# Sparse attention: a head's value products one turn later, with wide tiles for every other turn's transposed probabilities

## The chip, the cores and the metric

The kernel runs on one core of one Trainium2 chip. The metric is device time in microseconds, the median of several executions. The profile is of one further execution, with the time of every instruction on every engine of the core. TensorE appears in it twice: PE for its matmuls and transposes, PEld for its weight loads. DVE is VectorE, ACT is ScalarE, POOL is GpSimd, SP is SyncE, which here issues DMAs.

## The reference

One decoder layer for 512 tokens of width 1024: a feed-forward block, a token mixer, a second feed-forward block, each with norms and a residual. The mixer adds a native sparse attention (NSA, 8 heads of 64 in two groups) and a dilated attention. The change lies in the NSA part alone. Cut to what matters there:

```python
# s: scaled scores with ALiBi, masked; per head a selected and a window branch
p, _ = masked_softmax(s, mask)          # both branches: all earlier keys, since 512 tokens
o_slc = einsum('bgrqk,bgqkd->bqgrd', p_slc, v_slc)
o_win = banded_attention(q, k_win, v_win, ...)
g = sigmoid(gates)
o_nsa = g[..., 0:1] * o_cmp + g[..., 1:2] * o_slc + g[..., 2:3] * o_win
```

With 512 tokens all blocks of 64 keys are selected and the window holds every earlier key, so both branches are a causal softmax attention over 512 keys, with keys and values of their own. A third branch, over 31 compressed keys, is small.

## The kernel before, in words

All matrix work is done in float32r with an operand split into a rounded part ("hi") and its rest ("lo"): `split` (lines 106 to 108) casts on ACT (L107) and subtracts on DVE (L108). A projection multiplies hi by hi, hi by lo and lo by hi (L130, L131, L132).

The NSA stage is the loop of `nsa` (from L1034). It has 16 items, one for each head and branch (`heads`, L1031: four pairs of heads, two halves, two branches), and it walks them in turns, with one item entering in each turn:

- Turn n, scores: `hb_scores` multiplies queries by keys (L724, L725) into three PSUM banks of the kind S, of 512, 384 + 128 and 256 columns, adds the bias and takes the maximum on DVE (L730), and exponentiates on ACT (L731) into three SBUF tiles.
- Turn n + 2 (`LAG` = 2), probabilities: `hb_probs` scales the item's rows by gate over denominator (ACT L969, POOL L971), transposes them on PE in three blocks (L980, into a PSUM bank of the kind T: 512, 384 + 128 and 256 columns), and splits each block into hi and lo (L984, so L107 and L108), in two of the eight SBUF slots `PT`, each 128 x 512. An item takes six of the eight.
- The same turn n + 2, products: after the scores of the item that enters, `hb_values` multiplies values by the transposed probabilities (L995), for each of the four key blocks first with hi, then with lo, into the one PSUM bank of the kind V. After an item's second branch comes the compressed branch's product (L1061), and `fold` copies and adds the bank into the output (ACT L1003, DVE L1004), which frees the bank V.
- Beside them run a projection for every fourth turn (L130 to L132 into a bank F) and `fillers`: every third turn one projection of the merge gates (`merge_unit`), stored to DRAM.

PSUM has eight banks: three S, two T, one V, two F. So a block's transposes need the bank of the block before the last one, once ACT and DVE have read it, and a group of scores that of three groups back.

The Python order is not the order of the engines. When the program is built, a scheduler lists each engine's instructions: of those whose inputs it reckons ready it takes the one written earliest, so a thing written later fills the holes of what is written before. On the chip each engine then takes its list as it stands and waits on semaphores. The order rows below are those lists.

The tiles `NN` are three SBUF slots of 128 x 1024. Before, they hold token sums in the first feed-forward block, and then, in the dilated part behind NSA, pairs of weight rows for sums made ahead (`mixer_sums`: loads L466, DVE sums L449, stores L470).

Of the kernel before, what the change touches and what calls it, by code (L numbers as in the profile page):

```python
# [13 lines left out]
F32R = mybir.dt.float32r  # L14
# [7 lines left out]
P = 128  # L22
D = 1024
S = 512
# [7 lines left out]
LAG = 2  # L32
# [28 lines left out]
class Layer:  # L61
# [896 lines left out]
                self.softmax_rows(pt[n][:, o:o + ncol], b[:, o:o + ncol], w[:, S - ncol:S], st[:, 0, t:t + 1], st[:, 1, t:t + 1])  # L958
        return st, pt

    def hb_probs(self, st, pt, gate):

        nc = self.nc
        self.gated(st[:, 1], NT, gate)
        for t in (3, 2, 0, 1):
            n, o = self.PLACE[t]
            pp = pt[n][:, o:o + (t + 1) * P]
            if t == NT - 1:
                nc.scalar.mul(pp, pp, st[:, 1, t:t + 1])  # L969
            else:  # L970
                nc.gpsimd.tensor_scalar(pp, pp, st[:, 1, t:t + 1], None, op0=OP.mult)  # L971
        out = {}
        for kbs in ((0,), (1, 3), (2,)):
            b = self.bank("T")
            ncols = 0
            for kk in kbs:
                _, o = self.TPLACE[kk]
                for t in range(kk, NT):
                    pn, po = self.PLACE[t]
                    nc.tensor.transpose(b[:, o + (t - kk) * P:o + (t - kk + 1) * P],  # L980
                                        pt[pn][:, po + kk * P:po + (kk + 1) * P], self.ident)
                    ncols += P
            hi, lo = self.slot("PT", F32R)[:, 0:ncols], self.slot("PT", F32R)[:, 0:ncols]
            self.split(hi, lo, b[:, 0:ncols])  # L984
            for kk in kbs:
                _, o = self.TPLACE[kk]
                c = slice(o, o + (NT - kk) * P)
                out[kk] = hi[:, c], lo[:, c]
        return out
# [16 lines left out]
    def nsa(self, fillers):  # L1006
        nc = self.nc
        ident = lambda v: v
        r = self.wcols([(C_KC, 256)])
        src = [r[:, :, 0:P], r[:, :, P:2 * P]]  # L1010
        r2 = self.wcols([(C_KS, P), (C_KW, P)])
        src2 = [r2[:, :, 0:P], r2[:, :, P:2 * P]]
        early = []
        for s, tag in zip(src + src2, "FFSV"):
            w = self.wslots(s, "SP") if tag == "V" else None
            early.append(self.proj_T(s, self.bank(tag), (0, 2 * P), w))
            if len(early) in (2, 3):
                self.pending.pop(0)()
        for n, (b, w) in enumerate(early):
            self.proj_T(None, b, (2 * P, S), w)  # L1020
        rows = [self.block_rows(b) for b, _ in early[:2]]
        kw = early[3][0]
        vw = self.v_weights()
        kparts = [self.k_parts(early[2][0], ident)]
        gs = [self.blocks(0, rows[0])]
        kparts.append(self.k_parts(kw, ident))
        gs.append(self.blocks(1, rows[1]))
        self.v_nsa(vw)
        early = self.hidden_early(0)
        self.oh, self.ol = [], []  # L1030
        heads = [(i, half, br) for i in range(4) for half in range(2) for br in range(2)]  # L1031
        qs, cmps, ws, live = {}, {}, {}, {}
        probs = {}
        for n in range(len(heads) + LAG):  # L1034
            if n < len(heads) and n % 4 == 0:
                i = n // 4
                b, _ = self.proj_T(self.wcols([(i * 64, 64), (256 + i * 64, 64)]))
                qs[i] = self.q_parts(b, ident)
                if i:
                    cmps[i] = self.cmp_pair(i, qs[i])  # L1040
            m = n - LAG
            if m >= 0:
                i, half, br = heads[m]
                probs[m] = self.hb_probs(*live.pop(m), self.gate[:, :, (i + 4 * half) * 3 + 1 + br])
            if n < len(heads):
                i, half, br = heads[n]
                h = i + 4 * half
                if br == 0:
                    ws[h] = self.slot("W")
                    nc.vector.tensor_scalar(ws[h], self.dm, -(2.0 ** -(h + 1)), None, op0=OP.mult)  # L1050
                kb, ka = kparts[br]
                live[n] = self.hb_scores(qs[i][half], ka[half], kb, half, ws[h])
            if m >= 0:
                i, half, br = heads[m]
                if br == 0:
                    out = self.bank("V")
                    if half == 0:
                        of = self.slot("of")
                self.hb_values(probs.pop(m), br, half, out, br == 0)
                if br == 1:  # L1060
                    nc.tensor.matmul(out, self.vcs[half], cmps[i], start=False, stop=True, skip_group_check=True)  # L1061
                    self.fold(of, half, out[0:64], out[64:128])
                    if half == 1:
                        hi, lo = self.slot("x", F32R), self.slot("x", F32R)
                        self.split(hi, lo, of)
                        self.oh.append(hi)
                        self.ol.append(lo)
            if n < 2:
                self.hidden(n, gs[n], early)
                if n == 0:  # L1070
                    early = self.hidden_early(1)
                else:
                    hid = self.gelu()
            if n == 2:
                self.compressed(hid)
                cmps[0] = self.cmp_pair(0, qs[0])
            fillers()
# [465 lines left out]
```

## Time and profile before

| | |
|---|---|
| median of three runs | 1134.36 us (1134.22 to 1134.58) |
| the profiled execution's own time | 1135.51 us |
| its span, first to last instruction | 1133.7 us |
| outside the span | 1.8 us |
| granted TensorE clock, mean | 0.999 |
| NSA loop, from the first scores to the last value products | about 398 to 533 us of the span |
| instructions of L995, and the first and the last | 128, at 416.1 and 532.5 us |
| transposes L980, and the first and the last | 160, at 413.7 and 530.9 us |

In the rows of a timeline the first column is the start in us of the span, the second the length; an entry in square brackets is the time that the engine sat idle before the instruction, and whose end let it go. A merged row (x2, x4) spans its instructions.

### The profile page before, as it was taken

To read this page: it belongs to the slowest core of one execution; us is meant where nothing else is said; L and a number is where in the kernel's file an instruction comes from. 1 tells how busy PE (TensorE), PEld (TensorE's weight loads), DVE (VectorE), ACT (ScalarE), POOL (GpSimd) and SP (SyncE) were. 2 spreads that over 40 slices of the span, in tenths; PEclk is the share of its full clock that TensorE was granted. 3 is DMA by queue.
4 is the path that set the end of the run, shared out by engine and by line. 5 is a ranking of instruction groups with operands and counts; after the bars stand their busy time and mean duration, and the time that the engine had idled before them with its cause. 6 is when DMAs were issued, how large, how long until landed. Compare 5 with 4: busy or idle time off the path is not lost.

```text
span 1133.7 us, 18456 instructions
## 1 busy us (share of the span) xinstructions
PE 1119.2 (99%) x6921; PEld 1001.7 (88%) x6921; DVE 907.2 (80%) x1563; ACT 638.1 (56%) x1145; POOL 76.8 (7%) x112
## 2 busy tenths in 40 slices
PE   9999999999999999999999999999999999999997
PEld 7889999998888987778888998787989999998886
DVE  6989999879676889687665687986778888979774
ACT  5435555567563788677565634645445555557562
POOL 1000000000012033343000000000000000000000
PEclk9999999999999999999999999999999999999999
DMA  9996665588763542111476758683233424357862
GB/s 320 328 305 194 182 209 173 155 273 287 266 204 96 176 131 85 54 40 56 140 251 224 253 177 292 210 290 118 66 121 122 131 86 127 124 170 239 285 224 84
DMA packets 152908, 206.01 MB, mean 182 GB/s; under 512 B 19794, under 2 KB 97906, under 8 KB 152564
## 3 DMA queue, kind: packets, MB, share of 16 engines
q1 hardware_dynamic: 152816, 204.85, 55.7%
q8 instruction: 54, 0.88, 0.3%
q14 instruction: 34, 0.28, 0.1%
q10 hardware_dynamic: 4, 0.00, 0.0%
HBM read 165.45 MB, written 39.37 MB: 181 GB/s over the span
## 4 chain that ended last, share of the span: by engine, by line
PE 89%; DVE 5%; ACT 2%; issue 1%; DMA 1%; POOL 1%; SPq 0%; POOLq 0%; DVEq 0%; ACTq 0%
PE pb_F L132 11%; PE pb_F L130 11%; PE pb_F L131 11%; PE pb_S L132 8%; PE pb_S L131 8%; PE pb_S L130 8%; PE pb_T L130 6%; PE pb_T L132 6%; PE pb_T L131 6%; PE pb_V L131 3%; PE pb_V L130 3%; PE pb_V L132 3%; PE pb_V L995 2%; PE pb_T L980 1%; DVE SP_s L730 1%
## 5 line engine op out<-in xcount | busy, mean ns | idle before, releaser
L107 ACT CAST whi<-raw 128x1024 fp32r<-128x1024 f32 (+1 forms) x215 | 219.9, 1023 | 251.9 <-issue 68.2
L108 DVE TENSOR_TENSOR wlo<-raw,whi 128x1024 fp32r<-128x1024 f32 (+1 forms) x215 | 255.0, 1188 | 94.9 <-ACT whi L107 91.3
L130 PE MATMUL pb_F<-xh_t,whi 128*128 128x512 f32 (+1 forms) x392 | 142.7, 364 | 0.4 <-ACT whi L107 0.4
L132 PE MATMUL pb_F<-xh_t,wlo 128*128 128x512 f32 (+1 forms) x392 | 141.6, 361 | 0.5 <-DVE wlo L108 0.5
L131 PE MATMUL pb_F<-xl_t,whi 128*128 128x512 f32 (+1 forms) x392 | 141.8, 362 | 0.0
L107 ACT CAST whi<-tmp_t 128x1024 fp32r<-128x1024 f32 x51 | 53.5, 1048 | 60.9 <-PE pb_S L131 22.0
L132 PEld LDWEIGHTS pb_F<-xh_t,wlo 128*128 128x128 f32 x392 | 74.1, 189 | 10.8 <-DVE wlo L108 1.0
L130 PEld LDWEIGHTS pb_F<-xh_t,whi 128*128 128x128 f32 x392 | 74.1, 189 | 10.4 <-ACT whi L107 0.6
L131 PEld LDWEIGHTS pb_F<-xl_t,whi 128*128 128x128 f32 x392 | 74.2, 189 | 9.6
L108 DVE TENSOR_TENSOR wlo<-tmp_t,whi 128x1024 fp32r<-128x1024 f32 x51 | 62.4, 1223 | 25.2 <-ACT whi L107 23.9
L130 PE MATMUL pb_S<-xh_t,whi 128*128 128x256 f32 (+1 forms) x240 | 73.2, 305 | 0.0
L132 PE MATMUL pb_S<-xh_t,wlo 128*128 128x256 f32 (+1 forms) x240 | 73.0, 304 | 0.0
L131 PE MATMUL pb_S<-xl_t,whi 128*128 128x256 f32 (+1 forms) x240 | 73.0, 304 | 0.0
L130 PE MATMUL pb_T<-xh_t,whi 128*128 128x256 f32 (+1 forms) x184 | 54.5, 296 | 0.0
L132 PE MATMUL pb_T<-xh_t,wlo 128*128 128x256 f32 (+1 forms) x184 | 54.3, 295 | 0.0
L131 PE MATMUL pb_T<-xl_t,whi 128*128 128x256 f32 (+1 forms) x184 | 54.3, 295 | 0.0
L152 POOL TENSOR_TENSOR rs_t<-rs_t,mhalf_t 128x1 f32<-128x1 f32 x24 | 17.5, 727 | 542.7 <-DVE rs_t L148 542.7
L971 POOL TENSOR_SCALAR SP_s<-SP_s,st_t 128x384 f32<-128x384 f32 (+2 forms) x48 | 45.8, 970 | 107.1 <-DVE st_t L907 77.3
L131 PEld LDWEIGHTS pb_S<-xl_t,whi 128*128 128x128 f32 x240 | 45.9, 191 | 1.9
L130 PEld LDWEIGHTS pb_S<-xh_t,whi 128*128 128x128 f32 x240 | 45.9, 191 | 1.9
L132 PEld LDWEIGHTS pb_S<-xh_t,wlo 128*128 128x128 f32 x240 | 45.9, 191 | 1.9
L108 DVE TENSOR_TENSOR PT_s<-pb_T,PT_s 128x512 fp32r<-128x512 f32 (+1 forms) x72 | 39.2, 559 | 6.3 <-ACT PT_s L107 5.6
(822 smaller groups left out, 3363.8 us busy)
## 6 DMA issues: line engine op xcount, KB each, us to landing
raw<-in_ffn_w_up_dram SPq DMA_DIRECT2D x36, 512.0 KB, 5.3
raw<-in_w_in_dram SPq DMA_DIRECT2D x18, 1024.0 KB, 5.7
raw<-in_ffn_w_gate_dram SPq DMA_DIRECT2D x35, 512.0 KB, 4.9
raw<-in_ffn_w_down_dram SPq DMA_DIRECT2D x14, 1024.0 KB, 5.7
raw<-tdram SPq DMA_DIRECT2D x14, 1024.0 KB, 5.2
NN_s<-in_ffn_w_down_dram SPq DMA_DIRECT2D x22, 512.0 KB, 5.0
tdram<-NN_s SPq DMA_DIRECT2D x22, 512.0 KB, 3.9
raw<-in_ffn_w_down_dram SPq DMA_DIRECT2D x6, 768.0 KB, 5.8
```

The costliest lines, as they stand in the source:

```text
L107: self.last_cast = self.nc.scalar.copy(dsthi, src).ins
L108: self.last_rest = self.nc.vector.tensor_sub(dstlo, src, dsthi.bitcast(F32)).ins
L130: mm(out, lhi, rhi, start=start, stop=False, skip_group_check=skip)
L131: mm(out, lhi, rlo, start=False, stop=False, skip_group_check=skip)
L132: mm(out, llo, rhi, start=False, stop=stop, skip_group_check=skip)
L152: nc.gpsimd.tensor_tensor(out=r, in0=v, in1=self.mhalf, op=OP.pow)
L730: nc.vector.tensor_tensor_reduce(p, s, w, -1.0, FLOOR, OP.add, OP.min, st_m)
L971: nc.gpsimd.tensor_scalar(pp, pp, st[:, 1, t:t + 1], None, op0=OP.mult)
L980: nc.tensor.transpose(b[:, o + (t - kk) * P:o + (t - kk + 1) * P], pt[pn][:, po + kk * P:po + (kk + 1) * P], self.ident)
L995: self.nc.tensor.matmul(out[:, kk * P:S], v, pp, start=first and kk == 0 and pi == 0, stop=False, skip_group_check=True)
```

## The change

The value products of an item are written one turn later, behind the next item's transposes and scores, so the loop has one turn more. Since the transposed probabilities of two items are now alive together, every other item (the first, the third, and so on) puts its hi and lo side by side in the three wide `NN` tiles; the others keep the `PT` slots.

```diff
-    def hb_probs(self, st, pt, gate):
+    def hb_probs(self, st, pt, gate, wide):
...
-            hi, lo = self.slot("PT", F32R)[:, 0:ncols], self.slot("PT", F32R)[:, 0:ncols]
+            if wide:
+                both = self.slot("NN", F32R, (P, D))
+                hi, lo = both[:, 0:ncols], both[:, S:S + ncols]
+            else:
+                hi, lo = self.slot("PT", F32R)[:, 0:ncols], self.slot("PT", F32R)[:, 0:ncols]
...
-        for n in range(len(heads) + LAG):
+        for n in range(len(heads) + LAG + 1):
...
             m = n - LAG
-            if m >= 0:
+            if 0 <= m < len(heads):
                 i, half, br = heads[m]
-                probs[m] = self.hb_probs(*live.pop(m), self.gate[:, :, (i + 4 * half) * 3 + 1 + br])
+                probs[m] = self.hb_probs(*live.pop(m), self.gate[:, :, (i + 4 * half) * 3 + 1 + br], m % 2 == 0)
...
                 live[n] = self.hb_scores(qs[i][half], ka[half], kb, half, ws[h])
+            m -= 1
             if m >= 0:
                 i, half, br = heads[m]
                 if br == 0:
```

The same instructions stand in both programs. PE's list differs only inside the NSA loop, some 640 matmuls of 6,921; those of DVE and ACT likewise; POOL's by one memset; SP's by three loads. Lines behind the change carry higher numbers: L995 is now L999, L1061 is L1066.

PE, the fifth item. Before, from the last transpose of its first block (bank pb_T_5065) to the first product that reads that block's hi (PT_s_5070):

```order
L980 MATMUL pb_T_5065<-ident_t_61,SP_s_4925 128x128
L980 MATMUL pb_T_5074<-ident_t_61,SP_s_4927 128x128
L980 MATMUL pb_T_5074<-ident_t_61,SP_s_4926 128x128
L980 MATMUL pb_T_5074<-ident_t_61,SP_s_4925 128x128 x2
L724 MATMUL pb_S_5175<-KA_s_4205,Q_s_4851 128x256
L725 MATMUL pb_S_5175<-KB_s_4201,Q_s_4851 128x256
L131 MATMUL pb_F_5197<-xl_t_3671,whi_5193 128x512
L132 MATMUL pb_F_5197<-xh_t_3670,wlo_5194 128x512
L130 MATMUL pb_F_5197<-xh_t_3670,whi_5193 128x512
L131 MATMUL pb_F_5197<-xl_t_3671,whi_5193 128x512
L995 MATMUL pb_V_5115<-PT_s_5070,V_s_4259 128x512
```

After, the end of the stretch before the same products. NN_s_5049, NN_s_5057 and NN_s_5063 hold the fifth item's three blocks, transposed some rows above this piece; pb_T_5113 and pb_T_5122 are the sixth item's banks:

```order
L132 MATMUL pb_F_5177<-xh_t_3670,wlo_5174 128x512
L980 MATMUL pb_T_5113<-ident_t_61,SP_s_5007 128x128
L130 MATMUL pb_F_5177<-xh_t_3670,whi_5173 128x512
L980 MATMUL pb_T_5113<-ident_t_61,SP_s_5008 128x128
L980 MATMUL pb_T_5113<-ident_t_61,SP_s_5007 128x128
L980 MATMUL pb_T_5113<-ident_t_61,SP_s_5006 128x128
L980 MATMUL pb_T_5122<-ident_t_61,SP_s_5008 128x128
L980 MATMUL pb_T_5122<-ident_t_61,SP_s_5007 128x128
L980 MATMUL pb_T_5122<-ident_t_61,SP_s_5006 128x128 x2
L999 MATMUL pb_V_5161<-NN_s_5049,V_s_4259 128x512 x2
L999 MATMUL pb_V_5161<-NN_s_5057,V_s_4288 128x384 x2
L999 MATMUL pb_V_5161<-NN_s_5063,V_s_4317 128x256 x2
```

The fifth item's products have moved behind the sixth item's transposes, and now stand in one piece.

PE, the fourth item. Its third block takes the bank that its first block had. Before, the rows behind the last transpose of the first block (pb_T_4995) up to the first of the third (pb_T_5013):

```order
L724 MATMUL pb_S_5161<-KA_s_4205,Q_s_4851 128x512
L725 MATMUL pb_S_5161<-KB_s_4201,Q_s_4851 128x512
L995 MATMUL pb_V_4947<-PT_s_4919,V_s_4317 128x256
L995 MATMUL pb_V_4947<-PT_s_4911,V_s_4346 128x128
L995 MATMUL pb_V_4947<-PT_s_4912,V_s_4346 128x128
L980 MATMUL pb_T_5004<-ident_t_61,SP_s_4787 128x128
L980 MATMUL pb_T_5004<-ident_t_61,SP_s_4786 128x128
L980 MATMUL pb_T_5004<-ident_t_61,SP_s_4785 128x128 x2
L995 MATMUL pb_V_4947<-PT_s_5000,V_s_4259 128x512
L724 MATMUL pb_S_5166<-KA_s_4205,Q_s_4851 128x384
L725 MATMUL pb_S_5166<-KB_s_4201,Q_s_4851 128x384
L980 MATMUL pb_T_5013<-ident_t_61,SP_s_4786 128x128
```

After, from the last transpose of the first block (pb_T_4980) to the first of the third (pb_T_4998):

```order
L980 MATMUL pb_T_4980<-ident_t_61,SP_s_4772 128x128
L980 MATMUL pb_T_4989<-ident_t_61,SP_s_4774 128x128
L980 MATMUL pb_T_4989<-ident_t_61,SP_s_4773 128x128
L980 MATMUL pb_T_4989<-ident_t_61,SP_s_4772 128x128 x2
L999 MATMUL pb_V_5028<-NN_s_4896,V_s_4288 128x384
L999 MATMUL pb_V_5028<-NN_s_4902,V_s_4317 128x256 x2
L999 MATMUL pb_V_5028<-NN_s_4896,V_s_4346 128x128 x2
L724 MATMUL pb_S_5086<-KA_s_4172,Q_s_4837 128x256
L725 MATMUL pb_S_5086<-KB_s_4168,Q_s_4837 128x256
L980 MATMUL pb_T_4998<-ident_t_61,SP_s_4773 128x128
```

Less PE work stands between the two users of the bank than before.

SP, at the end of the loop. Before (raw are weights for the dilated part, gdram the fillers' stores, tdram the store of finished sums):

```order
L682 DMA raw_6306<-in_w_in_dram 128x8x256
L1086 DMA gdram_3872<-ring_s_5529 128x512
L1086 DMA gdram_3872<-ring_s_5837 128x512
L1086 DMA gdram_3872<-ring_s_6043 128x512
L682 DMA raw_6356<-in_w_in_dram 128x8x256
L682 DMA raw_6358<-in_w_in_dram 128x8x256
L470 DMA tdram_72<-NN_s_6340 128x1024
```

After, the same place:

```order
L682 DMA raw_6282<-in_w_in_dram 128x8x256
L1091 DMA gdram_3872<-ring_s_5504 128x512
L1091 DMA gdram_3872<-ring_s_5804 128x512
L1091 DMA gdram_3872<-ring_s_6010 128x512
L466 DMA NN_s_6316<-in_ffn2_w_down_dram 128x1024
L466 DMA NN_s_6317<-in_ffn2_w_down_dram 128x1024
L682 DMA raw_6332<-in_w_in_dram 128x8x256
L466 DMA NN_s_6484<-in_ffn2_w_down_dram 128x1024
L682 DMA raw_6334<-in_w_in_dram 128x8x256
```

Three loads of the NN tiles have come here from the end of the first feed-forward block, since the tiles are in use until the last wide item's products are done.

## The prediction

> **What bounds the kernel now.** I read the page's first part, then the windows around the NSA loop, then PEld's groups inside that loop, and last the timeline at three waits.
>
> ```profile
> PE 1119.2 (99%) x6921; PEld 1001.7 (88%) x6921; DVE 907.2 (80%) x1563; ACT 638.1 (56%) x1145; POOL 76.8 (7%) x112
> ```
>
> The windows (columns: PE, PEld, DVE, ACT, POOL busy, granted clock, DMA share, GB/s) are the whole loop, a dense stretch of it, and the dilated part behind it:
>
> ```profile
> 396.00:535.00 139.00, 137.46 (x786) 111.71 (x784) 114.42 (x338) 106.50 (x256) 48.41 (x54) 1.00 0.26 77
> 440.00:460.00 20.00, 19.66 (x117) 15.59 (x116) 17.97 (x60) 18.21 (x47) 11.14 (x12) 1.00 0.20 66
> 535.00:560.00 25.00, 25.00 (x118) 20.90 (x117) 16.66 (x36) 14.47 (x31) 1.04 (x2) 1.00 0.37 127
> ```
>
> TensorE is the bound, and a matmul's record covers short waits, so PE's 1.5 us of idle in the loop understates them. The weight loads show more. Their groups in the window 396 to 535 us (busy, mean ns, then idle before them and its releasers):
>
> ```profile
> L995 PEld LDWEIGHTS pb_V<-PT_s,V_s 128*128 128x128 f32 x128 | 21.1, 188 | 8.1 <-ACT PT_s L107 4.0 <-DVE PT_s L108 1.4 <-DVE of_s L1004 0.7
> L980 PEld LDWEIGHTS pb_T<-ident_t,SP_s 128*128 128x128 f32 x160 | 18.2, 141 | 4.4 <-DVE PT_s L108 1.8 <-PE pb_F L130 0.6 <-issue 0.4
> L724 PEld LDWEIGHTS pb_S<-KA_s,Q_s 128*128 128x128 f32 x64 | 12.1, 189 | 3.2 <-DVE st_t L730 1.6 <-issue 0.7 <-DVE Q_s L717 0.2
> ```
>
> The products L995 wait most: 4.0 us for casts (hi), 1.4 us for rests (lo), 0.7 us for the bank V, 6.1 us together. The transposes wait 1.8 us for a bank T, the scores 1.6 us for DVE's L730, which frees a bank S. One such wait, the fifth item's first product, on PEld, on PE and on ACT:
>
> ```profile
> 453.27 0.19 PEld L131 LDWEIGHTS pb_F<-xl_t,whi 128*128 128x128 f32 x1
> 453.92 0.19 PEld L995 LDWEIGHTS pb_V<-PT_s,V_s 128*128 128x128 f32 x1 [0.46 <-ACT PT_s L107]
> 454.03 0.19 PEld L132 LDWEIGHTS pb_F<-xh_t,wlo 128*128 128x128 f32 x1
> ```
> ```profile
> 453.04 0.40 PE L132 MATMUL pb_F<-xh_t,wlo 128*128 128x512 f32 x1
> 453.27 0.39 PE L130 MATMUL pb_F<-xh_t,whi 128*128 128x512 f32 x1
> 453.50 0.39 PE L131 MATMUL pb_F<-xl_t,whi 128*128 128x512 f32 x1
> 453.95 0.47 PE L995 MATMUL pb_V<-PT_s,V_s 128*128 128x512 f32 x1
> 454.26 0.39 PE L132 MATMUL pb_F<-xh_t,wlo 128*128 128x512 f32 x1
> ```
> ```profile
> 452.50 0.58 ACT L1003 COPY of_s<-pb_V 64x512 f32<-64x512 f32 x1
> 453.10 0.59 ACT L107 CAST PT_s<-pb_T 128x512 fp32r<-128x512 f32 x1
> 453.58 0.62 ACT L731 ACTIVATE SP_s<-SP_s,st_t 128x384 f32<-128x384 f32 x1
> ```
>
> Matmuls of 512 columns start 0.23 us apart (453.04, 453.27, 453.50). From 453.50 to 454.26 are 0.76 us for two, 0.30 us lost for 0.46 us of idle on PEld. So two thirds of a PEld wait are lost, and all of L995's are worth about 0.67 x 6.1 = 4.1 us. The weight load behind the waiting one came after it, at 454.03. The Trainium skill (TensorE: Matmul & The Clock Gate, "Step-by-step: what each phase is for") says that PE's window pulls weight loads ahead of matmuls in flight. If that reached past a load that waits, the next load, 0.11 us here, would be hidden and the price 0.19 us, not 0.30; by it the gains below would be 1.4 us, not 2.3. The row decides for 0.30.
>
> **The change part by part.** No instruction is added or removed, and PE's list differs in the loop alone. So only waits change.
>
> *Products against their casts (gain).* The spacing of PE's matmuls in a stretch without a wait:
>
> ```profile
> 439.28 0.39 PE L725 MATMUL pb_S<-KB_s,Q_s 128*128 128x512 f32 x1
> 439.51 0.33 PE L724 MATMUL pb_S<-KA_s,Q_s 128*128 128x384 f32 x1
> 439.68 0.34 PE L725 MATMUL pb_S<-KB_s,Q_s 128*128 128x384 f32 x1
> 439.85 0.22 PE L724 MATMUL pb_S<-KA_s,Q_s 128*128 128x128 f32 x1
> 439.91 0.27 PE L725 MATMUL pb_S<-KB_s,Q_s 128*128 128x128 f32 x1
> 440.02 0.33 PE L724 MATMUL pb_S<-KA_s,Q_s 128*128 128x256 f32 x1
> 440.19 0.28 PE L725 MATMUL pb_S<-KB_s,Q_s 128*128 128x256 f32 x1
> 440.31 0.40 PE L130 MATMUL pb_F<-xh_t,whi 128*128 128x512 f32 x1
> ```
>
> That is 0.23 us for 512 columns (439.28 to 439.51), 0.17 for 384, 0.12 for 256 (440.19 to 440.31) and 0.11 for 128 (439.91 to 440.02). In PE's lists I count the matmul work between a block's last transpose and the first product that reads it, at this spacing, for the 48 blocks (16 items of three). A hi part that waits looks like this one, with 0.55 us of work behind its transposes:
>
> ```profile
> 435.57 0.19 PEld L995 LDWEIGHTS pb_V<-PT_s,V_s 128*128 128x128 f32 x1 [0.25 <-ACT PT_s L107]
> ```
>
> Before, 20 of 48 hi parts have under 1.1 us of work between, and none over 3.1. After, 11 have under 1.1, and 13 over 3.5. The list is therefore only half of what the title says: the scheduler still fills holes with products as soon as it reckons them ready. I let the 4.0 us shrink with the near ones: 4.0 x 9/20 = 1.8 us saved (bounds 0 and 4.0, since waits like the one at 453.92 come from ACT's queue with 1.6 us of work between). Lo parts under 1.7 us fall from 14 to 3: 1.4 x 11/14 = 1.1 us. The bank V: in four items before, at most 2.1 us of work stands between L1061 and the next user, in one after: 0.7 x 3/4 = 0.5 us. Together 3.4 us on PEld, times 0.67: 2.3 us.
>
> *Transposes against their bank (cost).* What leaves the place between two blocks brings their transposes closer. A bank T of 512 columns:
>
> ```profile
> 492.53 0.38 PE L980 MATMUL pb_T<-ident_t,SP_s 128*128 128x128 f32 x2
> ```
> ```profile
> 493.56 0.69 DVE L108 TENSOR_TENSOR PT_s<-pb_T,PT_s 128x512 fp32r<-128x512 f32 x1 [0.22 <-ACT PT_s L107]
> ```
> ```profile
> 493.70 0.42 PEld L980 LDWEIGHTS pb_T<-ident_t,SP_s 128*128 128x128 f32 x4
> 494.31 0.20 PEld L980 LDWEIGHTS pb_T<-ident_t,SP_s 128*128 128x128 f32 x2 [0.19 <-DVE PT_s L108]
> ```
>
> Here 1.45 us of work stood between and 0.19 us was missing, so such a bank needs about 1.6 us. Before, two are under that, both at 1.45. After, five are: 1.22, 1.30 (the fourth item, shown above), 1.41, 1.46 and 1.58. The shortfalls are 0.38 + 0.30 + 0.19 + 0.14 + 0.02 = 1.0 against 0.3 us: 0.7 us more (bounds: 0, if ACT and DVE come earlier than in these rows; 2.6, if in two of five of the banks of the second rival the cast comes late).
>
> *Scores against their bank (cost).* The group of 512 columns that ends with the L725 at 439.28 leaves its bank to the group that starts here:
>
> ```profile
> 440.75 0.19 PEld L724 LDWEIGHTS pb_S<-KA_s,Q_s 128*128 128x128 f32 x1 [0.24 <-DVE st_t L730]
> ```
>
> With 1.26 us of work between it lost 0.1 us, so I take 1.35 us as the need. Before, this is the shortest of its kind; after, two stand at 0.80 and 0.98: 0.55 + 0.37 - 0.09 = 0.8 us more (bounds 0 and 1.5).
>
> *SP's list (no cost).* The three NN loads wait at SP for the last wide products, near the end of the loop, and the two raw loads stand behind them. Before:
>
> ```profile
> 530.19 9.54 SPq L682 DMA_DIRECT2D raw<-in_w_in_dram  x2
> ```
> ```profile
> 547.89 1.06 ACT L107 CAST whi<-raw 128x1024 fp32r<-128x1024 f32 x1 [1.97 <-PE pb_F L131]
> ```
> ```profile
> 544.68 1.41 DVE L449 TENSOR_TENSOR NN_s<-NN_s 128x512 f32<-128x512 f32 x2
> ```
> ```profile
> raw<-in_w_in_dram SPq DMA_DIRECT2D x18, 1024.0 KB, 5.7
> NN_s<-in_ffn_w_down_dram SPq DMA_DIRECT2D x22, 512.0 KB, 5.0
> ```
>
> The first raw tile is issued at 530.19 and cast at 547.89, 17.7 us later, and lands in 5.7 us. The sums that read NN come at 544.68, 14.5 us after that time, and an NN load lands in 5.0 us. If all three came one after another ahead of the raw tile (15 us) and PE's cover of some 12 us were gone, that would cost up to 9 us; I give it 2 in 100. DVE's and ACT's lists change as PE's does, with the same work.
>
> *The sum.* -2.3 + 0.7 + 0.8 = -0.8 us. The profiled execution took 1135.51 us, 1.8 us more than its span of 1133.7, and lies 1.15 us above the median of 1134.36; it would come to 1134.7, the median to **1133.6**. What a measurement of this kernel can tell from no change is about 0.2%, or 2.27 us.
>
> **The rivals.**
>
> *All of L995's waits go and nothing takes their place* (faster). Then the median is 1134.36 - 4.1 = 1130.3. For it: the 13 blocks with over 3.5 us cannot wait for a cast, and in the loop DVE is busy 114 and ACT 107 of 139 us, so they are not full. Against it: 11 blocks stay near. Chance 0.25.
>
> *The bank waits grow by more than the product waits shrink* (slower). The mechanism is the pair of T banks: the third block of an item needs the first one's, 1.6 us after its transposes. After the change 14 banks of 512 columns have at most 1.8 us between, before 10. In the dense stretch ACT is busy 18.21 of 20 us, and the cast has to stand behind an exponential of 0.62 us (453.58). If casts come that much later than in the row above, the 14 lack about 0.6 us each where the 10 now lack little more than the 1.8 us that the view shows, so up to 0.6 x 14 - 1.8 = 6.6 us; with half of them so, 3.3 us more, which leaves 3.3 + 0.8 - 2.3 = +1.8, and with two thirds 2.6 us, or 1137.0. It decides from half on. The Trainium skill (Perfetto Trace Analysis, "Optimization Strategy") has the rule for it: the same gap over and over on the engine that should be full can mean too few SBUF or PSUM buffers. The change adds room in SBUF and none in PSUM; by that rule the gap stays. Chance 0.13.
>
> *The change hardly does what it says* (no change). The scheduler reorders, and in PE's list the last head's products end within 1 us of work of where they did. Then 1134.4. Chance 0.17. My forecast has 0.45.
>
> **How the numbers follow.** The likeliest is 1133.6. The low end is the first rival's 1130.3; the high end takes both costs at their upper bounds with the gain as it is (-2.3 + 2.6 + 1.5 = +1.8, so 1136.2). Left out are half of the slower rival, SP, and a little below. Faster by over 0.2% (below 1132.1): the first rival and the lower tail of the forecast, 0.27. Slower (above 1136.6): 0.13. The rest, 0.60, is within 0.2%.
>
> **What would show it.** In PEld's groups of the same window L999 should show about 2.7 us of named waits in place of 6.1, L980 about 2.5 behind L108 in place of 1.8, L724 about 2.4 behind L730 in place of 1.6; the rest of the span should keep its lengths, and no wait for NN or raw should appear behind 530 us. L999 near zero with the others as they were means the first rival; L980 above 5 us the second; all as before the third.

## The result: 6.3 us slower, and the profile after

| | before | after |
|---|---|---|
| median, runs on the same chip | 1134.47 us (1133.88 to 1135.14) | 1140.76 us (1139.15 to 1143.11) |
| profiled execution, its span | 1135.51, 1133.7 us | 1141.66, 1139.9 us |

The ratio is 1.0056 (95% interval 1.0046 to 1.0066). The forecast was 1133.6 with a range up to 1136.2, and 0.60 of its chances lay on no change: it was wrong.

Where it arose. PE's list differs in the NSA loop alone, so the same matmul can be looked up in both traces by its number. Just before the loop's first changed matmul the execution after is 0.18 us ahead, at its last 5.96 us behind (538.61 for 532.65 us), and at the end of the span 6.15. These are the windows of the kernel after, with the stretch 520 to 540 added (busy PE, PEld, DVE, ACT, POOL, granted clock, DMA share, GB/s):

```profile
396.00:535.00 139.00, 132.30 (x758) 108.06 (x756) 110.29 (x334) 104.36 (x253) 50.13 (x54) 0.99 0.23 67
440.00:460.00 20.00, 17.57 (x102) 14.43 (x102) 16.05 (x53) 15.51 (x41) 7.03 (x6) 0.91 0.21 66
520.00:540.00 20.00, 17.67 (x98) 13.69 (x99) 11.92 (x31) 11.78 (x27) 6.59 (x8) 1.00 0.23 78
535.00:560.00 25.00, 24.84 (x117) 20.32 (x116) 13.85 (x20) 10.59 (x17) 0.00 (x0) 1.00 0.68 224
```

PE is idle for 2.4 us of 440 to 460 (0.34 before), and the granted clock there is 0.91 (1.00 before). PEld's groups of the window 396 to 540:

```profile
L980 PEld LDWEIGHTS pb_T<-ident_t,SP_s 128*128 128x128 f32 x160 | 18.4, 144 | 12.9 <-POOL SP_s L971 5.7 <-issue 2.3 <-DVE NN_s L108 1.7
...
L724 PEld LDWEIGHTS pb_S<-KA_s,Q_s 128*128 128x128 f32 x64 | 12.1, 189 | 2.9 <-DVE st_t L730 1.1 <-issue 0.9 <-DVE Q_s L717 0.2
L999 PEld LDWEIGHTS pb_V<-NN_s,V_s 128*128 128x128 f32 x64 | 10.8, 201 | 2.9 <-ACT NN_s L107 1.8 <-DVE of_s L1008 0.4
L999 PEld LDWEIGHTS pb_V<-PT_s,V_s 128*128 128x128 f32 x64 | 10.4, 190 | 1.3 <-ACT PT_s L107 0.4
```

The products' named waits are 2.6 us, as foreseen (2.7, from 6.1). The scores' are 1.1 (2.4 foreseen). The transposes' waits behind the rest L108 are 3.5 us (2.5 foreseen): 1.7 for NN, shown above, and in the list of waits 1.2 for PT and 0.6 for CP. New is the first entry of L980: 5.7 us for POOL's scaling L971, a releaser that PEld's groups of before do not name at all. All but 0.2 us of it comes at two places. The first is the sixth item (item 5, counted from 0); the timeline after, then before:

```profile
451.93 0.16 DVE L907 TENSOR_TENSOR st_t<-st_t,gate_t 128x4 f32<-128x4 f32 x1
...
452.28 3.17 POOL L971 TENSOR_SCALAR SP_s<-SP_s,st_t 128x384 f32<-128x384 f32 x3 [7.37 <-DVE st_t L906]
...
454.16 0.14 PEld L980 LDWEIGHTS pb_T<-ident_t,SP_s 128*128 128x128 f32 x1 [1.88 <-POOL SP_s L971]
...
455.50 1.36 PEld L980 LDWEIGHTS pb_T<-ident_t,SP_s 128*128 128x128 f32 x7 [1.09 <-POOL SP_s L971]
...
456.84 2.06 PEld L999 LDWEIGHTS pb_V<-NN_s,V_s 128*128 128x128 f32 x7
```
```profile
450.85 0.16 DVE L907 TENSOR_TENSOR st_t<-st_t,gate_t 128x4 f32<-128x4 f32 x1
...
451.20 5.78 POOL L971 TENSOR_SCALAR SP_s<-SP_s,st_t 128x384 f32<-128x384 f32 x6 [6.62 <-DVE st_t L907]
...
457.07 0.86 PEld L980 LDWEIGHTS pb_T<-ident_t,SP_s 128*128 128x128 f32 x8
```

Read them as a chain. An item's rows are scaled by gate over denominator before they are transposed: DVE's three gate steps (L905, L906, L907) come first, then POOL's three scalings, and the first transpose needs POOL's second, the second transpose POOL's third. Before, the scalings of item 5 begin at 451.20 (the merged row holds items 5 and 6) and the transposes come at 457.07, 3.2 us after the third had ended. After, POOL begins 1.1 us later, but PE is there already when its matmul before is done, at 452.4 (452.21 and 0.23 us of spacing). It stands 1.7 us, runs one transpose and one matmul, stands 1.0 us more, and the products L999 of the item before, whose last input DVE had finished at 453.6, are queued behind. The second place is item 14, again after, then before:

```profile
524.47 0.15 DVE L907 TENSOR_TENSOR st_t<-st_t,gate_t 128x4 f32<-128x4 f32 x1
...
524.79 5.44 POOL L971 TENSOR_SCALAR SP_s<-SP_s,st_t 128x384 f32<-128x384 f32 x6 [3.99 <-DVE st_t L905]
...
526.67 0.14 PEld L980 LDWEIGHTS pb_T<-ident_t,SP_s 128*128 128x128 f32 x1 [1.88 <-POOL SP_s L971]
...
527.57 0.75 PEld L980 LDWEIGHTS pb_T<-ident_t,SP_s 128*128 128x128 f32 x7 [0.65 <-POOL SP_s L971]
```
```profile
517.76 2.73 POOL L971 TENSOR_SCALAR SP_s<-SP_s,st_t 128x384 f32<-128x384 f32 x3 [1.07 <-DVE st_t L907]
...
525.15 0.91 PEld L980 LDWEIGHTS pb_T<-ident_t,SP_s 128*128 128x128 f32 x7
```

Before, POOL was 4.7 us early here (517.76 + 2.73 = 520.49, for 525.15). The pauses of item 5 also cost clock. Windows of 2 us after:

```profile
452.00:454.00 2.00, 0.60 (x4) 0.28 (x3) 1.72 (x8) 1.90 (x4) 1.72 (x2) 1.00 0.00 0
454.00:456.00 2.00, 1.06 (x5) 0.75 (x6) 0.66 (x3) 0.00 (x0) 1.45 (x2) 0.81 0.00 0
456.00:458.00 2.00, 2.00 (x9) 1.81 (x9) 0.90 (x3) 1.56 (x4) 0.00 (x0) 0.50 0.00 0
458.00:460.00 2.00, 2.00 (x13) 1.87 (x12) 1.24 (x4) 1.12 (x5) 0.00 (x0) 0.84 0.00 0
```

Behind them the clock stands at 0.50, and PE takes 0.21 us for a transpose (0.11 at full clock), so the seven transposes need 1.36 us where those at 527.57 need 0.75. Against the spacing of the prediction's rows, PE loses 1.7 + 1.0 us in the pauses of item 5, 1.5 at half clock, and 1.7 + 0.7 in the pauses of item 14: 6.6 us, of which the rest of the loop gives 0.5 back. That is the loss.

Why the chain was met there shows in the lists, with the spacings of PE and DVE's durations (0.66 us for 512 columns, 0.54, 0.41, 0.27 for 384, 256, 128, 0.16 for a small step):

| | PE work from the item's last score to its first transpose | DVE work from its last maximum to its last gate step |
|---|---|---|
| item 5, before and after | 14.7, 11.0 us | 6.5, 8.8 us |
| item 14, before and after | 12.2, 10.7 us | 4.2, 10.9 us |

The products that left the place between an item's scores and its transposes let the transposes move up; and in DVE's new list rests (L108) and bias work (L730) stand ahead of the gate steps. Why the scheduler set them there was not followed. Item 5 loses 3.7 + 2.3 = 6.0 us of a margin of 3.2, item 14 1.5 + 6.7 = 8.2 of 4.65. The deficits are 2.8 and 3.5 us; the pauses that PE shows are 2.7 and 2.4. At items 9 and 13 the same count gives deficits of 1.3 and 1.0 us, and PE lost 0.2 us or less there: the count finds tight places, but gives their size only roughly.

### The profile page after: what moved, and what is told of

The parts are those of the page before. It is cut to its first block, busy times and chain, and to the rows that moved or that the text cites. A ratio compares the mean times of both kernels' runs of the same rounds, so it can differ in the third digit from the quotient of the medians.

```text
span 1139.9 us, 18451 instructions
## 1 busy us (share of the span) xinstructions
PE 1119.8 (98%) x6921; PEld 1002.6 (88%) x6921; DVE 905.9 (79%) x1563; ACT 637.8 (56%) x1145; POOL 78.5 (7%) x112
## 4 chain that ended last, share of the span: by engine, by line
PE 89%; DVE 4%; ACT 3%; DMA 1%; issue 1%; POOL 1%; SPq 0%; POOLq 0%; DVEq 0%; ACTq 0%
PE pb_F L132 11%; PE pb_F L130 11%; PE pb_F L131 11%; PE pb_S L130 8%; PE pb_S L131 8%; PE pb_S L132 8%; PE pb_T L130 6%; PE pb_T L132 6%; PE pb_T L131 6%; PE pb_V L130 3%; PE pb_V L131 3%; PE pb_V L132 3%; PE pb_T L980 1%; PE pb_V L999 1%; PE pb_S L724 1%
## 5 line engine op out<-in xcount | busy, mean ns | idle before, releaser
L108 DVE TENSOR_TENSOR wlo<-raw,whi 128x1024 fp32r<-128x1024 f32 (+1 forms) x215 | 255.5, 1190 | 101.9 <-ACT whi L107 99.1
L108 DVE TENSOR_TENSOR wlo<-tmp_t,whi 128x1024 fp32r<-128x1024 f32 x51 | 62.4, 1223 | 25.2 <-ACT whi L107 23.9
L971 POOL TENSOR_SCALAR SP_s<-SP_s,st_t 128x384 f32<-128x384 f32 (+2 forms) x48 | 47.5, 1005 | 110.7 <-DVE st_t L907 55.8
L730 DVE CUSTOM_DVE_ANT_0 SP_s<-pb_S,W_s 128x128 f32<-128x128 f32 (+2 forms) x92 | 37.8, 441 | 6.7 <-PE pb_S L725 4.7
```

Of the source, the lines that this page charges most:

```text
L108: self.last_rest = self.nc.vector.tensor_sub(dstlo, src, dsthi.bitcast(F32)).ins
L730: nc.vector.tensor_tensor_reduce(p, s, w, -1.0, FLOOR, OP.add, OP.min, st_m)
```

## The experiments

The theory, A: the loss is the chain from the gate steps over POOL's scaling to the transposes at these places. Rivals: B, the banks T and S, with casts that come late (the prediction's slower rival); C, the wide tiles themselves. In the kernels with an early scaling, the code below it moves down some lines: their transposes are L984 and their products L1003.

**The gate and the scaling one turn earlier.**

```diff
+            if 2 < n <= len(heads):
+                i, half, br = heads[n - 1]
+                self.hb_scale(*live[n - 1], self.gate[:, :, (i + 4 * half) * 3 + 1 + br])
             m = n - LAG
```

`hb_scale` holds the lines L964 to L971 of `hb_probs`; items 0 and 1 keep theirs. On the kernel after:

> Theory A (the gate steps L905 to L907 and POOL's scaling L971 of items 5 and 14 come after PE has reached these items' transposes): with the gate and the scaling of items 2 to 15 written one turn earlier, DVE has 3.5 us (item 5) and 5.7 us (item 14) of work between the item's last maximum and its last gate step, where the changed kernel has 8.8 and 10.9; the transposes stay where they were (11.9 and 10.8 us of PE work behind the item's last score, 11.0 and 10.7 in the changed kernel). PEld's wait for POOL (5.7 us in the changed kernel) falls under 0.7 us, and the time to 1133 to 1135 us. Rival B (banks T and S, casts late behind exponentials): nothing of it is touched, so 1139 to 1141. Rival C (the wide tiles themselves): 1139 to 1141.

Measured: 1134.89 us, ratio to the kernel before 0.9998 (0.9988 to 1.0008). The named wait for POOL is 1.2 us in three pieces, over the 0.7 expected; but the scaling ended 1.7 us or more ahead of the second transpose in every item, so there POOL's name stands for another releaser. Theory A stands, B and C as causes of the 6 us fall. On the kernel before:

> The kernel before with the same early gate and scaling. Theory A: the kernel before has no wait for POOL, so there is nothing to take away: 1133.5 to 1135. If early scaling is a gain of its own, whatever the products do, it falls by as much as the changed kernel does with it, some 6 us, to about 1128.

Measured: 1135.42 us, 1.0008 (0.9999 to 1.0018), 0.4 us above theory A's range. Early scaling is no gain of its own; it only repairs what the change broke.

**The gate steps alone earlier**, with `self.gated(...)` in that place and the scaling left in `hb_probs`:

> The changed kernel with only DVE's three gate steps (L905 to L907) of items 2 to 15 written one turn earlier; POOL's and ACT's scaling stays where it was written. Theory A1 (the link is DVE's list: POOL stands idle until the last gate step has run): DVE has 3.5 and 5.7 us of work between the last maximum and the last gate step of items 5 and 14 (8.8 and 10.9 in the changed kernel), POOL starts that much sooner, its wait on PEld is under 0.7 us and the time 1134 to 1136 us. Theory A2 (the link is POOL's or ACT's scaling itself, where it stands or how long it takes): 1139 to 1141 us.

Measured: 1135.33 us, 1.0010 (1.0001 to 1.0019), as A1 says: the link is DVE's list. The wait for POOL that is left, 2.1 us in five pieces of at most 0.6, is more than the 0.7 expected, yet POOL ended 2.7 us or more ahead of the second transpose in all items but the first (0.05): in the others the name again stands for another releaser.

**Items 5 and 14 alone**, so `if n - 1 in (5, 14)` in the first diff:

> The changed kernel with the early gate and scaling for items 5 and 14 alone. Their transposes stand even a little sooner behind the scores than in the changed kernel (10.5 us both, for 11.0 and 10.7), all other items as there. If the whole loss lies at these two places, the time is 1134.5 to 1136.5 us, and the granted clock, which falls to 0.50 behind the first pause of the changed kernel, stays at 1.00 there. If the loss comes from all the items with late gates (9, 10 and 13 too), it stays over 1137.

Measured: 1134.80 us, 1.0000 (0.9990 to 1.0009). In this execution the transposes of items 5 and 14 begin sooner, at 450.75 and 519.77 us. PEld's group of the transposes, and windows at the two places:

```profile
L984 PEld LDWEIGHTS pb_T<-ident_t,SP_s 128*128 128x128 f32 x160 | 17.8, 141 | 8.5 <-issue 3.0 <-DVE NN_s L108 1.3 <-DVE PT_s L108 1.2
```
```profile
450.00:452.00 2.00, 1.84 (x13) 1.67 (x14) 1.94 (x6) 1.98 (x6) 0.27 (x1) 1.00 0.00 0
452.00:454.00 2.00, 2.00 (x16) 1.83 (x15) 1.92 (x6) 2.00 (x7) 0.00 (x0) 1.00 0.00 0
...
520.00:522.00 2.00, 1.85 (x16) 1.53 (x15) 1.44 (x5) 1.56 (x4) 1.20 (x1) 1.00 0.00 0
```

POOL is gone from the first three releasers, PE is idle for at most 0.16 us in any of these windows, and the clock stays at 1.00. Two items of sixteen carry the whole loss.

**The wide tiles alone**, the products in their old turn (`m -= 1` and the extra turn taken out):

> The wide tiles for every other item, but the products in the turn where the kernel before has them. Theory A and rival B: 1134 to 1135.5, no wait for POOL, since transposes stand as far behind the scores as before (12.2 us at the least). Rival C: the wide tiles cost by themselves, 1137 to 1141.

Measured: 1136.18 us, 1.0011 (1.0002 to 1.0021), no named wait for POOL. Rival C falls as the cause of 6 us; the 1.3 us over the kernel before (at most 2.4 by the interval) is more than I expected. In its trace PE loses 1.3 us more in front of the products than before, and these wait 7.1 us by name for ACT's casts (4.0 before); why the casts come later was not followed.

**Late products, written ahead of the next item's transposes**, that is, the block under `if m >= 0` moved ahead of `hb_probs`:

> The changed kernel, but an item's products, still one turn later, written ahead of the next item's gate, scaling and transposes instead of behind its scores. PE then has at least 12.4 us of work between an item's last score and its first transpose (10.7 in the changed kernel), 14.0 for item 5 and 13.0 for item 14, and DVE 4.2 and 7.4 us before their last gate step. Theory A: no wait for POOL, some of the waits for casts gone: 1132.5 to 1134.5. Rival B: as many transposes as before stand close on each other (3 under 1.6 us where the changed kernel has 9), so it also says at most 1135; rival C (wide tiles): 1139 to 1141.

Measured: 1135.41 us, 1.0004 (0.9994 to 1.0013), no named wait for POOL, with the same lateness and the same tiles. The time is 0.9 us over what was expected: the products' waits for ACT's casts are back (2.9 us for tiles PT, 1.9 for NN), so nothing is gained either.

**A rule from the lists, tried forward.** The block put between `hb_probs` and `hb_scores`:

> The changed kernel, with an item's late products written ahead of the next scores instead of behind them (still behind the next item's gate, scaling and transposes). A rule worked out from the lists is tried on it: take the time by which POOL was early in the kernel before (3.2 us for item 5, 4.8, 4.9 and 4.65 for 9, 13 and 14), add the PE work and subtract the DVE work by which the lists differ from those of the kernel before. For the changed kernel that gives -2.9, -1.3, -1.0 and -3.6 us, and PE stood 2.8, 0.1, 0.1 and 2.4. Here it gives -1.1 (item 5: transposes 3.5 us sooner, gate 0.8 us later), -1.3, -1.0 and -3.6: a pause of about 1.1 us at item 5 with the clock at 1.00 behind it, and the same 2.4 at item 14, so 1137 to 1139.5 us. If lateness as such costs the 6 us, 1140 to 1142.

Measured: 1137.87 us, 1.0024 (1.0014 to 1.0033), the clock 1.00 at both places. PE lost 0.4 us at item 5 and 2.4 at item 14: the rule has the places, and is off by 0.7 us at the first. At the second it counts 3.6, as for the kernel after; the 2.4 was expected from that kernel's pause, not from the rule. Next, the products of items 4 and 13 back in their old turn:

> The changed kernel with the products of items 4 and 13 alone back in their old turn; these are the products that stood queued behind the waiting transposes of items 5 and 14. By the rule from the lists the waits stay (-2.9 us for item 5 as before, -2.9 for item 14, which was -3.6), so 1139 to 1141 us, and the clock falls behind the pause of item 5. If what costs is that ready products of these two items stand behind the waiting transposes, the time is 1135 to 1137.

Measured: 1140.59 us, 1.0049 (1.0034 to 1.0064), as expected, but by luck, since it did not come in the expected way. Item 5 paused 1.7 us instead of 2.7 and kept its clock, since the products of item 4 now stood between its first two transposes: here the rival had a point. Item 14 paused 1.7 us instead of 2.4 (2.9 by the rule). What was saved was lost at another place (rows of its timeline):

```profile
526.58 0.40 POOL L1099 TENSOR_SCALAR_AFFINE_SELECT of_s<-dm_t 128x256 f32<-128x256 f32 x1
...
527.01 0.29 DVE L1118 TENSOR_SCALAR W_s<-of_s 128x256 f32<-128x256 f32 x1 [4.49 <-POOL of_s L1099]
...
528.75 0.20 PEld L980 LDWEIGHTS pb_T<-ident_t,SP_s 128*128 128x128 f32 x2 [2.83 <-DVE NN_s L108]
```

POOL's L1099, for the dilated part, stands behind the last item's scalings; DVE waits for it 4.5 us in its list with item 14's rests behind it, and PE for these. Then only the odd items' products late:

```diff
-            m -= 1
-            if m >= 0:
+            for m in [k for k in (n - LAG - 1, n - LAG) if 0 <= k < len(heads) and n - LAG - k == (k % 2 == 1)]:
```

> The changed kernel with only the odd items' products late, gate and scaling where they were. The rule from the lists gives 3.8 us for item 5 and 0.6 for item 14 (no pause), -0.6 and -1.4 for items 9 and 13, where the changed kernel with -1.3 and -1.0 lost 0.1 each: no pause over 1 us, the clock at 1.00 throughout the loop, 1134.5 to 1136.5 us. If late products cost by their number, half of the loss: 1137 to 1138.5.

Measured: 1135.02 us, 1.0001 (0.9992 to 1.0011), the wait for POOL 0.3 us, no pause over 1 us. Half of the late products cost nothing, so the cost does not go by their number. The same with the early gate and scaling:

> Only the odd items' products one turn later, with the early gate and scaling; the wide tiles as in the changed kernel. The search for a gain: 12 of 48 casts have under 1.1 us of work in front of their product (20 in the kernel before), 7 banks T under 1.6 us (2 before, 8 with all products late and the early gate). Theory A with the sum of the prediction: 1132.5 to 1134.5. If what the products save goes to the transposes' banks, as it did with all products late: 1134 to 1136.

Measured: 1136.21 us, 1.0014 (1.0005 to 1.0024), just above the second expectation: PE loses 0.8 us less in front of products and 0.4 more in front of transposes, and 1.2 more before projections and the small steps. No version beat the kernel before.

**The dose.** In the kernel before:

```diff
                 nc.gpsimd.tensor_scalar(pp, pp, st[:, 1, t:t + 1], None, op0=OP.mult)
+                nc.gpsimd.tensor_scalar(pp, pp, 1.0, None, op0=OP.mult)
```

> The kernel before with a second multiplication by 1.0 behind each of POOL's scalings, 2.8 us more per item in the chain to the transposes; PE's list is that of the kernel before. In its trace POOL ends 1.7 us ahead of the second transpose in item 0 and 3.2 us or more in all others. Theory A (what counts is this slack): only item 0 waits, by 1.1 us, so 1135 to 1136.5 us. If POOL's length is paid in every tight item (5, 13, 14, 15), 2.8 us each: 1142 to 1147.

Measured: 1145.90 us, 1.0108 (1.0091 to 1.0125), 9 us above theory A's range and inside the other's (1142 to 1147), but not by the other's mechanism. PEld's waits of this kernel (total, times, longest):

```profile
PEld pb_V L996 <- issue: 4.6, 1, 4.6
PEld pb_V L996 <- ACT PT_s L107: 3.9, 11, 0.8
PEld pb_T L981 <- POOL SP_s L972: 3.2, 2, 2.6
```

The tight items behave as theory A says: item 5 keeps 0.65 us of its 3.2, item 14 0.7 of 4.65, and neither stands. But item 0 lacked 2.6 us instead of 1.1, because POOL's six operations took 7.7 us there where they took 5.3 in item 5, and at the loop's end a single pause of 4.6 us comes from the neighbour just met (its timeline):

```profile
533.31 0.40 POOL L1095 TENSOR_SCALAR_AFFINE_SELECT of_s<-dm_t 128x256 f32<-128x256 f32 x1
533.74 0.29 DVE L1114 TENSOR_SCALAR W_s<-of_s 128x256 f32<-128x256 f32 x1 [5.03 <-POOL of_s L1095]
...
534.15 0.68 DVE L1005 TENSOR_TENSOR of_s<-pb_V,of_s 64x512 f32<-64x512 f32 x1
...
534.97 0.77 PE L996 MATMUL pb_V<-PT_s,V_s 128*128 128x512 f32 x1 [4.20 <-DVE of_s L1005]
```

DVE's fold and rests stand in its list behind an instruction that waits for POOL. A margin that holds for one user of an engine says nothing of the next one in its queue; and with both pauses the granted clock went to 0.50.

## Why the prediction was wrong, point by point

PE's time in the loop beyond the spacing of its matmuls, by what it lost the time in front of (worked out from the starts of PE's matmuls):

| us | products | transposes L980 | scores | others | all |
|---|---|---|---|---|---|
| before | 2.87 | 2.99 | 2.60 | 2.20 | 10.66 |
| after | 1.36 | 10.08 | 2.68 | 2.68 | 16.80 |
| after, items 5 and 14 scaled early | 0.54 | 5.27 | 2.68 | 2.63 | 11.12 |

- **What bounds the kernel**: right. TensorE is the bound and only its waits count.
- **Products, -2.3 us**: right in kind and size. With the two stops gone they lose 2.3 us less; in the kernel after 1.5 us less, since some of them run at half clock.
- **Transposes against their bank, +0.7 us (bounds 0 to 2.6)**: too small. With the stops gone L980 loses 2.3 us more than before, and this is where the products' gain went, and why the repaired versions measure 1134.8 to 1136.2 and not 1132. How much of it the banks take is open: the four largest pieces (0.32 to 0.52 us) stand behind a rest L108, the mechanism of the slower rival, but by name these waits grow only from 1.8 to 3.1 us (items 5 and 14 scaled early), while "issue", for which the profile names no releaser, grows from 0.4 to 3.0. No run took either away.
- **Scores against their bank, +0.8 us**: too large; 0.1.
- **SP's list, nothing**: right; no wait of PE for NN or raw behind 530 us.
- **The step that failed** is the one without a number: "DVE's and ACT's lists change as PE's does, with the same work", with the sum made only of waits that the trace of before already showed. The transposes have a second input, POOL's scaled rows. It showed no wait, so it was not priced; but it was hidden by a margin of 3.2 us at item 5 and 4.65 at item 14, and the change took from both sides of it: transposes up, gate steps back. Both margins could be read from the trace of before and both shifts from the lists.
- **The slower rival** had the sign and the wrong mechanism. The rule named with it, of the Trainium skill (Perfetto Trace Analysis, "Optimization Strategy"), that a gap which comes again and again can mean too few buffers, was put to no test, since no run gave the loop more banks. The gaps that cost the 6 us came twice, for a late input. In the rival's sum two thirds of 6.6 us are 4.4, so it should read +2.9 us, or 1137.3, and not +2.6; the forecast does not use it.
- **The clock** was in no term. The window 456 to 458 shows 0.50, worth 1.5 of the 6 us in this execution. The Trainium skill (TensorE: Matmul & The Clock Gate, "What's actually happening") says that a gate halves the clock after at least one idle window of about 3.4 us. The half agrees with 0.50; the idle time does not quite: the clock fell at 455.23 us, 0.75 us into the second pause, when PE had been idle for 2.5 of the 3.4 us before, with 0.3 us of work between the pauses.
- **Whether every execution has the fall** is open, since one was traced. Of the six of the kernel after, three show a mean granted clock of 0.999, as the kernel before does, and took 1139.2 to 1139.9 us; the others show 0.996 to 0.998 and took 1141.7 to 1143.1. This suggests that some 5 us of the loss are there without it.

## What to carry to other kernels

When a change moves work on a bound engine, price not only the waits that the profile shows but the margins of all inputs of what moves: when each was ready, and when it was used. Set against each margin what both lists move, the consumer's forward and the producer's back; a gate step of 0.16 us in a queue of rests can hold up the engine that matters. Look also at who stands next in each queue that gets later.

## What the runs showed of the hardware

Apart from its start and end, the granted clock fell to half at four places in the thirteen traces, each time for 3.41 us: from 455.23 us in the kernel after, from 529.10 with the products of items 4 and 13 put back, and from 415.02 and 534.49 with doubled scalings. Within a trace, the times from one switch of the clock to the next are whole multiples of 3.41 us; the 116.05 us from the clock's return to its second fall with doubled scalings (418.44 to 534.49) are 34 of them. So the clock changes on a grid here, and each trace can be cut along its own.

What PE's matmuls leave free in each such stretch is an estimate from their starts and spacings. The four stretches that end where the clock falls leave 2.5, 2.5, 2.5 and 3.4 us of 3.41 free; no other stretch between 40 and 1080 us of the thirteen traces leaves over 1.9. This tells apart pauses that look alike. Item 5's pauses in the kernel after lie in one stretch up to the fall (451.82 to 455.23). Item 14's, 1.7 and 0.7 us, lie on two sides of a border at 526.91, and the clock stayed at 1.00; so it did behind 1.7 us alone (item 5 with two items' products put back, 1.9 us free in all). Where between 1.9 and 2.5 us the limit lies was not tried, and the borders lie at other times in other traces, so the same pauses need not always cost the same clock.
